# A decoder layer on one core: two output blocks by halves, a later conditioning product, and work moved to other phases

## The chip, the core and the metric

The kernel runs on one core of a Trainium2 chip. The core has TensorE (PE, with its weight loads shown apart as PEld), VectorE (DVE), ScalarE (ACT), GpSimd (POOL), SyncE (SP), which here issues most of the DMAs, and 16 DMA engines. Each engine takes its instructions in a fixed order, so an instruction that waits holds up all that stand behind it on that engine. The metric is the time of one execution on the device, in microseconds (us). The kernel before took 1681.6 us (median of 3 runs, 1681.38 to 1685.16).

## The reference

One layer of a decoder trunk is computed in float32 for 1024 prompt tokens and 8 requests of 8 tokens each, 1088 columns in all, with a model width of 1024:

```python
h = rms_norm(x, norm_mix) * (1 + sc) + sh            # sh, sc, gt = silu(c) @ w_ada_mix + b
P = h @ w_in                                         # RWKV-7, pooling and gate columns
merged = g_r * (rwkv(P) @ w_br_rwkv) + g_p * (pool(P) @ w_br_pool)
x = x + gt * (merged @ w_out)
sh, sc, gt = split(silu(c) @ w_ada_mlp + b_ada_mlp, 3)
h = rms_norm(x, norm_mlp) * (1 + sc) + sh
x = x + gt * (square(relu(h @ w_ff1)) @ w_ff2)
y = rms_norm(x, norm_final)
```

## The kernel before

Activations lie in SBUF with channels on the partitions and the 1088 columns along the free axis; a row of blocks (`xr[0]` to `xr[7]`) is the residual stream. HF is 544, half of the columns, HQ is 272. A float32 product is built from three matmuls of rounded operands: every operand is split into a high part (`whi`, or the first tile of a pair `mr`, `hx`, `t`), made by ACT with a copy, and a low part (`wlo`, or the second tile), made by DVE or POOL with a subtraction. ACT, DVE and POOL thus work ahead of PE all the time, and a PSUM tile is free for PE only after one of them has read ("evicted") it.

The first part of the program (to about 790 us) makes the first norm, `w_in`, the recurrent heads and the pooling. The change touches the second part, the function `phase2`, which goes through these stages.

- **Merge** (`or_job`, eight blocks m). DVE evicts the branch product into `t`, POOL adds the other branch (L1369), ACT and DVE split the sum into the pairs `mg` (L1372, L1373). POOL then writes one element of `t` into the next residual tile and into the first conditioning tiles (`behind`, L1338), so that their loads can't be issued before.
- **Output product** (`out_job(m, i)`, i the half of the columns). A job has two halves of weights; half 0 uses `mg[0]` to `mg[3]`, half 1 uses `mg[4]` to `mg[7]`, with 24 matmuls of 272 columns each. The list `order` sets the sequence: job 0 half 0, job 0 half 1, job 1 half 0, and so on.
- **Conditioning** (`ada`, `ada_part`, L290). `silu(c) @ w_ada_mlp` is made in three groups of four pairs of tiles `hid<-in_w_ada_mlp`, 512 KB a tile. Its matmuls (`wc<-hid,sT`, 8 a pair) are put between those of the output product by a planner (`Pace`), which counts modelled nanoseconds of matmuls: a first pair comes after `gap + lead`, each other one after `gap`.
- **ff1**, as a product of halves with seven terms c (0 to 6) in place of eight. Each output unit j is a "pair" `u`, `o`. For the first eight units (`early`) the terms 0 and 1 are computed ahead, while the norm still makes the operands of the other five; their `u` and `o` are parked in DRAM and come back later. In this early phase the order of terms is: c=0 of units j and j+1, then c=1 of both, and c=1 is added into the same PSUM tile that c=0 filled, after ACT has copied it to `u` (L1530). After c=1 ACT makes `o` by Relu and Square (L1532, L1533) before it is parked.
- **ff2**, in groups of units with phases `ph` 0 to 2, also with seven terms. `spread` loads and splits the operands of coming terms; DVE adds each PSUM tile into accumulators (L1697). Afterwards `whole` adds the accumulators into the residual stream (`residual`, L1876, L1879), and the last quarter of the units goes through eight plain jobs (`ff2_jobs`, 36 matmuls each, evicted by L1876 too), whose operands `hidden` splits (L1758). Their PSUM tiles lie where those of the sums lay.
- The last norm and the stores.

PE's order is written out by these lists and the planner. The order on the other engines comes from a scheduler that runs on modelled times when the program is built, so a moved line can change the order of its neighbours too.

Of the kernel before, what the change touches and what calls it, by code (L numbers as in the profile page):

```python
# [9 lines left out]
F32 = mybir.dt.float32  # L10
# [126 lines left out]
class K:  # L137
# [1060 lines left out]
    def run(self):  # L1198
        tc, nc, io = self.tc, self.nc, self.io
        with ExitStack() as ctx:  # L1200
            self.cp = ctx.enter_context(tc.tile_pool(name="cp", bufs=1))
            self.wp = ctx.enter_context(tc.tile_pool(name="wp", bufs=2))
            self.hx = ctx.enter_context(tc.tile_pool(name="hx", bufs=1))
            dp = ctx.enter_context(tc.tile_pool(name="dp", bufs=1, space=DRAM))
            scratch = lambda n, k: [dp.tile([P, NT], F32, name=f"{n}{i}") for i in range(k)]
            self.d_bv, self.d_y = (scratch(n, 4) for n in ("d_bv", "d_y"))
            self.d_or, self.d_op = ([scratch(n + s, 4) for s in "hl"] for n in ("d_or", "d_op"))
            self.d_th, self.d_x = scratch("d_th", 16), scratch("d_x", 14)
            self.d_xr, self.d_hid = scratch("d_xr", 8), scratch("d_hid", 8)
            cut = lambda n: [[dp.tile([P, HF], F32, name=f"{n}{c}_{j}") for j in range(4 * NG)] for c in range(7)]  # L1210
            self.d_ch, self.d_cl = cut("d_ch"), cut("d_cl")
            self.d_u = [dp.tile([P, HF], F32, name=f"d_u{j}") for j in range(NE)]
            self.pc = ctx.enter_context(tc.tile_pool(name="pc", bufs=2, space=PSUM))
            self.part = self.cp.tile([P, NPAR], F32, name="part")
            nc.gpsimd.dma_start(self.part, io["par"])
            self.kct = self.cp.tile([P, NKC], F32, name="kct")
            nc.gpsimd.dma_start(self.kct, io["kc"])
            self.eps = self.cp.tile([P, 3], F32, name="eps")
            for i, v in enumerate((NORM_EPS, KK_EPS, GN_EPS)):
                nc.gpsimd.memset(self.eps[:, i:i + 1], v)  # L1220
            self.hp = self.cp.tile([P, 16], F32, name="hp")
# [103 lines left out]
    def phase2(self):  # L1325
# [15 lines left out]
        def ada():  # L1341
# [7 lines left out]
            for g in range(3):  # L1349
# [2 lines left out]
                    self.done.add("ada")  # L1352
                    yield lambda: ("hid", NE - 1) in self.done
                asb = p.tile([P, 512], F32, tag="wr2", bufs=4, name=self.nm("asb"))
                yield from self.ada_part("w_ada_mlp", g, tile, asb, self.aq, "b_mlp", (8 * g, 8 * g + 4), 6200, 2500, 13000 if g == 0 else 0)

        def or_job(m):
            S = {}
# [7 lines left out]

            def after():
                t = S["t"]
                nc.gpsimd.tensor_tensor(t, t, S["u"], op=ALU.add)  # L1369
                hi, lo = zip(*[MR() for _ in range(2)])  # L1370
                for i, s in enumerate(split):
                    nc.scalar.activation(hi[i], t[:, s], AF.Copy)  # L1372
# [97 lines left out]
        def pair_steps(j, early):  # L1470
# [13 lines left out]
            def prep(c):  # L1484
                def go():
                    if c == 0:
                        return self.halves(raw("a", 0, 0), False)
                    if c == 5:
                        if early == 2:
                            raw("a", 0, 0)  # L1490
                            S["u"], S["o"] = self.pair(p, "hid", 4, dt=F32)
                            nc.sync.dma_start(S["u"], self.d_u[j])
                            nc.sync.dma_start(S["o"], self.d_ch[0][j])
                        b, cc = raw("b", 1, 0), raw("c", 1, 1)
                        nc.vector.tensor_tensor(cc, b, cc, op=ALU.add)
                        d = raw("d", None, None)
# [20 lines left out]
            def run(c):  # L1517
                def go(w):
                    if c in (0, 1):
# [3 lines left out]
                        if c == 0:  # L1523
                            if early:
                                S["u"], S["o"] = self.pair(p, "hid", 4, dt=F32)
                            else:
                                S["u"], S["u1"] = self.pair(self.hx, "hx", 16, dt=F32)
                                S["o0"] = HX(F32)
                                S["o"] = S["o0"][:, :HF]
                            nc.scalar.activation(v2(S["u"]), v, AF.Copy)  # L1530
                        else:
                            nc.scalar.activation(v2(S["o"]), v, AF.Relu)  # L1532
                            nc.scalar.activation(S["o"], S["o"], AF.Square)  # L1533
                            if early:
                                nc.sync.dma_start(self.d_u[j], S["u"])
                                nc.sync.dma_start(self.d_ch[0][j], S["o"])
                        return
                    ps = self.ps2()
                    yield from product(ps, c, w, True, True)
# [5 lines left out]
                        nc.vector.tensor_tensor(v2(S["u"]), v2(S["u"]), v, op=ALU.add)  # L1545
                    elif c == 6:
                        nc.vector.tensor_tensor(v2(S["u1"]), v2(S["u"]), v, op=ALU.add)
                    elif c == 4:
                        o = S["o1"] = HX(F32)
                        nc.vector.tensor_tensor(v2(S["u"]), v2(S["u"]), v, op=ALU.add)  # L1550
# [27 lines left out]
            def apart(c, x, hi):  # L1578

                if early:  # L1580
                    if c:
                        nc.sync.dma_start(self.d_ch[c][j], x)
                    return
                nc.scalar.activation(hi.bitcast(F32R), x, AF.Copy)
                nc.vector.tensor_tensor(x.bitcast(F32R), x, hi, op=ALU.subtract)
# [128 lines left out]
        def ff2():  # L1714
            n = 0
            for i, (g, ph, (_, run, c)) in enumerate(sums):
                n = n + 1 if i and sums[i - 1][1] == ph else 0
                yield from run(made.pop(0))
                more()
                if ph == 0 and n == 1:  # L1720
                    spread(g, (4,))
                if ph == 0 and n == 4:
                    spread(g, (3,))
                if ph == 1 and n in (2, 5):
                    if g in after:
                        spread(after[g], (n // 3,))
                    else:
                        for m in range(n // 3 * 4, n // 3 * 4 + 4):
                            self.xr[m] = HX(F32)
                            nc.sync.dma_start(self.xr[m], self.d_xr[m])  # L1730
                if ph == 2 and n in (0, 2, 4):
                    if g in after:
                        spread(after[g], ((6, 5, 2)[n // 2],))
                    elif n == 2:
                        hidden(6)

        def whole():

            yield lambda: "sums" in self.done
            for mp in range(4):  # L1740
                (a1, a4), (a2, a3) = ACC[mp]
                for i, s in enumerate(split):
                    c0, n = s.start, s.stop - s.start
                    for h in range(2):
                        x = (a1, a3)[h] if i == 0 else (a2, a4)[h]
                        if h != i:
                            nc.vector.tensor_tensor(x, a4, x, op=ALU.subtract)  # L1747
                        self.residual(self.xr[2 * mp + h], self.aq[:, 16 + 2 * mp + h, :])(c0, n, x)
                yield 1500

        hid = {}

        def hidden(grp):
            for j in range(4):
                raw, hi, lo = self.row(p, "hid", 4), self.row(p, "mr", 16, F32R), self.row(p, "mr", 16, F32R)
                nc.sync.dma_start(raw, self.d_hid[4 * (grp - 6) + j])
                nc.scalar.activation(hi, raw, AF.Copy)
# [10 lines left out]
        for m in range(8):  # L1768
            order += U(or_job(m))
        for i in range(2):  # L1770
            for m in range(8):
                order += U(out_job(m, i))
        order2 = []
        for m, j in enumerate(ff2_jobs(6)):
            order2 += U(j)
# [231 lines left out]
```

## Time and profile before

| | |
|---|---|
| time, median of 3 runs | 1681.6 us (1681.38 to 1685.16) |
| profiled execution, its own time | 1687.4 us |
| its span, from first to last instruction | 1685.6 us |
| PE, PEld busy | 1615.4 us (96%), 1501.4 us (89%) |
| DVE, ACT, POOL busy | 1023.3 us (61%), 677.3 us (40%), 358.5 us (21%) |
| mean granted TensorE clock | 0.982 |
| HBM traffic | 198.15 MB read, 76.72 MB written, 163 GB/s over the span |

PE is busy nearly all the time, so the time can change by what PE waits, by the time in which its clock is not granted in full (a matmul then shows about twice its pitch), and hardly by anything else. In the rows of the profile a group is given as line, engine, operation and `out<-in`; brackets behind a row of the timeline hold the idle time of that engine just before it and what ended it. In rows of windows the granted clock stands as PEclk, 1.00 in full.

### The profile page before, as it was taken

The page shows a single profiled execution, that of the slowest core. Times are in us where ns is not written, and L with a number is a line of the kernel's source. Part 1 is how long each engine was busy: PE and PEld are TensorE (multiplying, and loading weights), DVE is VectorE, ACT ScalarE, POOL GpSimd, SP SyncE. Part 2 cuts the span into 40 slices and gives each one's busy share as a digit, 9 for nine tenths or more (in the row PEclk, how much of TensorE's full clock was granted, in tenths as well). Part 3 has the DMA queues.
Part 4 walks back from the last instruction along what each step waited for, and adds up shares of the span by engine and source line. Part 5 has one row for each costly group of instructions (what it writes and reads, how often), then busy time and mean ns, then how long its engine had stood idle before and what let it go on. Part 6 is the DMA issues. An engine that isn't in the chain of part 4 may idle for free. (4 is left out here: it accounts for less than half of the span.)

```text
span 1685.6 us, 35156 instructions
## 1 busy us (share of the span) xinstructions
PE 1615.4 (96%) x14331; PEld 1501.4 (89%) x14331; DVE 1023.3 (61%) x1674; ACT 677.3 (40%) x1262; POOL 358.5 (21%) x393
## 2 busy tenths in 40 slices
PE   6999999998999999999989989999999999999997
PEld 3989878886888789979979989999999999999897
DVE  5686556845674456334635596776655577677646
ACT  4543333344334333422324374444555554333122
POOL 3310110010000000001722234453322141311221
PEclk9999999999998999999989999999999999999999
DMA  9233413232423242475964446766555876574112
GB/s 335 98 114 133 141 55 119 100 103 71 126 89 105 69 147 80 146 279 199 335 236 163 149 138 227 239 235 229 199 205 193 321 233 211 164 259 135 45 44 107
DMA packets 128321, 277.17 MB, mean 164 GB/s; under 512 B 16640, under 2 KB 30976, under 8 KB 128160
## 3 DMA queue, kind: packets, MB, share of 16 engines
q1 hardware_dynamic: 120480, 253.03, 44.0%
q10 hardware_dynamic: 6048, 16.23, 2.8%
q0 software_dynamic: 1632, 5.67, 1.0%
q8 instruction: 113, 1.85, 0.4%
q14 instruction: 48, 0.39, 0.1%
HBM read 198.15 MB, written 76.72 MB: 163 GB/s over the span
## 5 line engine op out<-in xcount | busy, mean ns | idle before, releaser
L170 PE MATMUL mm<-hx,whi 128*128 128x362 f32 (+1 forms) x1920 | 511.5, 348 | 6.9 <-ACT px L565 2.9
L170 PEld LDWEIGHTS mm<-hx,whi 128*128 128x128 f32 x1920 | 337.0, 192 | 43.5 <-issue 18.6
L170 PE MATMUL pr<-mr,whi 128*128 128x272 f32 x1792 | 338.9, 288 | 4.5 <-DVE hx L1697 3.4
L170 PE MATMUL mm<-hx,wlo 128*128 128x362 f32 (+1 forms) x960 | 317.6, 331 | 0.0
L170 PEld LDWEIGHTS pr<-mr,whi 128*128 128x128 f32 x1792 | 281.7, 189 | 8.6 <-issue 8.3
L170 PE MATMUL pr<-mr,wlo 128*128 128x272 f32 x896 | 258.5, 289 | 0.0
L193 ACT ACTIVATE whi<-wraw 128x512 fp32r<-128x512 f32 x201 | 126.4, 629 | 290.1 <-PE mm L170 109.3
L170 PEld LDWEIGHTS mm<-hx,wlo 128*128 128x128 f32 x960 | 184.5, 192 | 0.0
L194 DVE TENSOR_TENSOR wlo<-wraw,whi 128x512 fp32r<-128x512 f32 x146 | 112.2, 769 | 111.0 <-ACT whi L193 108.9
L170 PE MATMUL pr<-hx,whi 128*128 128x272 f32 x896 | 170.6, 289 | 6.4 <-ACT hid L1530 5.4
L170 PEld LDWEIGHTS pr<-mr,wlo 128*128 128x128 f32 x896 | 169.2, 189 | 0.0
L170 PE MATMUL mm<-mr,whi 128*128 128x272 f32 (+4 forms) x736 | 156.4, 307 | 6.5 <-DVE hx L1697 3.7
L170 PEld LDWEIGHTS pr<-hx,whi 128*128 128x128 f32 x896 | 141.7, 190 | 7.9 <-ACT hid L1530 5.7
L194 POOL TENSOR_TENSOR wlo<-wraw,whi 128x512 fp32r<-128x512 f32 x55 | 79.5, 1446 | 273.7 <-ACT whi L193 267.2
L170 PEld LDWEIGHTS mm<-mr,whi 128*128 128x128 f32 x736 | 121.4, 192 | 15.1 <-issue 7.3
L193 ACT ACTIVATE whi<-wr 128x512 fp32r<-128x512 f32 x123 | 76.3, 627 | 142.3 <-PE pr L170 118.2
L170 PE MATMUL pr<-hx,wlo 128*128 128x272 f32 x448 | 129.6, 289 | 0.0
L170 PE MATMUL mm<-mr,wlo 128*128 128x272 f32 (+4 forms) x368 | 111.7, 303 | 0.0
L170 PEld LDWEIGHTS pr<-hx,wlo 128*128 128x128 f32 x448 | 85.0, 190 | 0.0
L170 PE MATMUL pr<-t,whi 128*128 128x272 f32 x448 | 84.6, 287 | 0.0
L194 DVE TENSOR_TENSOR wlo<-wr,whi 128x512 fp32r<-128x512 f32 x94 | 70.3, 750 | 22.6 <-ACT whi L193 22.6
L170 PEld LDWEIGHTS mm<-mr,wlo 128*128 128x128 f32 x368 | 70.8, 193 | 0.2
(377 smaller groups left out, 2618.7 us busy)
## 6 DMA issues: line engine op xcount, KB each, us to landing
wr<-in_w_ff SPq DMA_DIRECT2D x123, 256.0 KB, 3.5
wraw<-in_w_ff SPq DMA_DIRECT2D x85, 256.0 KB, 3.1
hid<-d_ch SPq DMA_DIRECT2D x80, 272.0 KB, 4.4
wraw<-in_w_in SPq DMA_DIRECT2D x68, 256.0 KB, 3.0
d_ch<-hx SPq DMA_DIRECT2D x52, 272.0 KB, 4.3
hid<-in_w_ada_mlp SPq DMA_DIRECT2D x24, 512.0 KB, 5.7
d_th<-px SPq DMA_DIRECT2D x22, 544.0 KB, 3.0
wt<-d_x SPq DMA_DIRECT2D x20, 544.0 KB, 4.1
```

The lines of the kernel that those rows point to most:

```text
L170: return self.nc.tensor.matmul(out, lhsT, rhs, **kw)
L193: nc.scalar.activation(hi, raw, AF.Copy)
L194: (nc.gpsimd if pool else nc.vector).tensor_tensor(lo, raw, hi.bitcast(F32), op=ALU.subtract)
```

## The change

Five edits, all in `phase2`:

1. Output product of the first column half: jobs 0 and 1 run by halves (both jobs' half 0, then both jobs' half 1), and the last merge addition (m = 7) is on DVE in place of POOL.
2. Conditioning: the lead of the first pair becomes 19000 (was 13000), the gap of the others 5600 (was 6200).
3. Early units: after c=1 ACT only copies PSUM to `o`; `u` and `o` are both parked in a buffer of their own (`d_u[0]`, `d_u[1]`); Relu and Square are done when the unit has come back, at term 6, and the finished `o` is stored to `d_ch[0]` at the combinations (one store a unit more).
4. ff2: the term 2 of the coming operands is spread in phase 0 in place of the end of phase 2, the others at other counts, and the splits of the plain jobs' operands come in two parts.
5. `whole`: the additions into the residual stream take their factors from a copy `gq`, which is first written from a value of the last accumulator, so that none of them can run before the last sum.

```diff
@@ scratch in DRAM @@
-            self.d_u = [dp.tile([P, HF], F32, name=f"d_u{j}") for j in range(NE)]
+            self.d_u = [[dp.tile([P, HF], F32, name=f"d_u{i}_{j}") for j in range(NE)] for i in range(2)]
@@ ada @@
-                yield from self.ada_part("w_ada_mlp", g, tile, asb, self.aq, "b_mlp", (8 * g, 8 * g + 4), 6200, 2500, 13000 if g == 0 else 0)
+                yield from self.ada_part("w_ada_mlp", g, tile, asb, self.aq, "b_mlp", (8 * g, 8 * g + 4), 5600, 2500, 19000 if g == 0 else 0)
@@ or_job, after @@
-                nc.gpsimd.tensor_tensor(t, t, S["u"], op=ALU.add)
+                (nc.vector if m == 7 else nc.gpsimd).tensor_tensor(t, t, S["u"], op=ALU.add)
@@ pair_steps, prep of term 5 when a unit returns @@
-                            nc.sync.dma_start(S["u"], self.d_u[j])
-                            nc.sync.dma_start(S["o"], self.d_ch[0][j])
+                            nc.sync.dma_start(S["u"], self.d_u[0][j])
+                            nc.sync.dma_start(S["o"], self.d_u[1][j])
@@ pair_steps, run of terms 0 and 1 @@
+                        elif early:
+                            nc.scalar.activation(v2(S["o"]), v, AF.Copy)
+                            nc.sync.dma_start(self.d_u[0][j], S["u"])
+                            nc.sync.dma_start(self.d_u[1][j], S["o"])
                         else:
                             nc.scalar.activation(v2(S["o"]), v, AF.Relu)
                             nc.scalar.activation(S["o"], S["o"], AF.Square)
-                            if early:
-                                nc.sync.dma_start(self.d_u[j], S["u"])
-                                nc.sync.dma_start(self.d_ch[0][j], S["o"])
...
                     elif c == 6:
                         nc.vector.tensor_tensor(v2(S["u1"]), v2(S["u"]), v, op=ALU.add)
+                        if early:
+                            relu2(S["o"])
@@ apart @@
                 if early:
-                    if c:
-                        nc.sync.dma_start(self.d_ch[c][j], x)
+                    nc.sync.dma_start(self.d_ch[c][j], x)
                     return
@@ ff2 @@
-                if ph == 0 and n == 1:
-                    spread(g, (4,))
-                if ph == 0 and n == 4:
-                    spread(g, (3,))
+                if ph == 0 and n in (0, 2, 5) and (n or g != GO[0]):
+                    spread(g, ({0: 2, 2: 4, 5: 3}[n],))
...
-                if ph == 2 and n in (0, 2, 4):
+                if ph == 2 and n in (0, 4):
                     if g in after:
-                        spread(after[g], ((6, 5, 2)[n // 2],))
-                    elif n == 2:
-                        hidden(6)
+                        spread(after[g], (6 - n // 4,))
+                    else:
+                        hidden(6, n // 2)
@@ whole @@
+            gq = gt
+            nc.vector.tensor_copy(gq[:, 0, 0:1], ACC[3][1][1][:, 0:1])
+            nc.vector.tensor_copy(gq, self.aq[:, 16:24, :])
...
-                        self.residual(self.xr[2 * mp + h], self.aq[:, 16 + 2 * mp + h, :])(c0, n, x)
+                        self.residual(self.xr[2 * mp + h], gq[:, 2 * mp + h, :])(c0, n, x)
@@ the list order @@
         for i in range(2):
-            for m in range(8):
-                order += U(out_job(m, i))
+            outs = [out_job(m, i) for m in range(8)]
+            if i == 0:
+                order += [(j, h) for h in range(2) for j in outs[:2]]
+            for j in outs[0 if i else 2:]:
+                order += U(j)
```

SP's rows at the change from the merge to the output product, before (a load `wraw` is a block of output weights, a `hid` a tile of conditioning weights, `d_xr` the store of a residual block):

```order
L182 DMA wraw_9327<-in_w_out 128x512
L182 DMA wraw_9371<-in_w_out 128x512
L290 DMA hid_9282<-in_w_ada_mlp 128x1024
L290 DMA hid_9285<-in_w_ada_mlp 128x1024
L290 DMA hid_9358<-in_w_ada_mlp 128x1024
L290 DMA hid_9360<-in_w_ada_mlp 128x1024
L1407 DMA d_xr_120<-hx_8816 128x544
```

The same place on SP with the change:

```order
L182 DMA wraw_9327<-in_w_out 128x512
L290 DMA hid_9349<-in_w_ada_mlp 128x1024
L290 DMA hid_9352<-in_w_ada_mlp 128x1024
L182 DMA wraw_9367<-in_w_out 128x512
L182 DMA wraw_9401<-in_w_out 128x512
L290 DMA hid_9428<-in_w_ada_mlp 128x1024
L290 DMA hid_9430<-in_w_ada_mlp 128x1024
L1407 DMA d_xr_120<-hx_8824 128x544
```

The second pair of conditioning tiles stands one weight block earlier, and the third no longer directly behind it.

ACT's rows in the early phase of ff1, before (L1397 makes the high parts of the norm's operands, the two L1530 copy the c=0 products of units 4 and 5, for which PE waits before it adds c=1):

```order
L1397 ACTIVATE mr_10857<-hx_9064 128x544
L1397 ACTIVATE mr_10860<-hx_9134 128x544
L1397 ACTIVATE mr_10863<-hx_9196 128x544
L1397 ACTIVATE mr_10866<-hx_9258 128x544
L1397 ACTIVATE t_10890<-hx_9196 128x544
L193 ACTIVATE whi_10945<-wr_1490_10943 128x512
L1530 ACTIVATE hid_10941<-pr_10916 128x544
L193 ACTIVATE whi_10978<-wr_1495_10976 128x512
L1530 ACTIVATE hid_10974<-pr_10949 128x544
```

The same place on ACT with the change:

```order
L1530 ACTIVATE hid_10945<-pr_10920 128x544
L1397 ACTIVATE mr_10814<-hx_9010 128x544
L1397 ACTIVATE mr_10829<-hx_8824 128x544
L1397 ACTIVATE mr_10832<-hx_8886 128x544
L1397 ACTIVATE mr_10835<-hx_8948 128x544
L1397 ACTIVATE mr_10838<-hx_9010 128x544
L1397 ACTIVATE mr_10862<-hx_9072 128x544
L1397 ACTIVATE mr_10865<-hx_9142 128x544
L1397 ACTIVATE mr_10868<-hx_9204 128x544
L1397 ACTIVATE mr_10871<-hx_9266 128x544
L193 ACTIVATE whi_10982<-wr_1495_10980 128x512
L1530 ACTIVATE hid_10978<-pr_10953 128x544
```

Unit 4's copy now stands ahead of nine of the `mr` copies; unit 5's copy still stands behind them.

DVE's rows at the end of the sums, before (L1697 with `pr_17743` reads the last sum's PSUM, L1747 and L1876 are `whole`, L1876 on `mm` evicts the first plain job):

```order
L1876 SCALAR_TENSOR_TENSOR hx_17361<-hx_15006,aq,hx_17361 128x480
L1697 TENSOR_TENSOR hx_15006<-hx_15006,pr_17743 128x544
L1758 TENSOR_TENSOR mr_17948<-hid_17946,mr_17947 128x1088
L1876 SCALAR_TENSOR_TENSOR hx_17359<-hx_14951,aq,hx_17359 128x544
L1747 TENSOR_TENSOR hx_15006<-hx_15005,hx_15006 128x544
L1876 SCALAR_TENSOR_TENSOR hx_17363<-hx_15006,aq,hx_17363 128x544
L1876 SCALAR_TENSOR_TENSOR hx_17249<-mm_17841,aq,hx_17249 128x364
```

The same place with the change (the lines L1699, L1750, L1761, L1882, L1885 are the old L1697, L1747, L1758, L1876, L1879), first from the last sum on, then up to the first job:

```order
L1699 TENSOR_TENSOR hx_15012<-hx_15012,pr_17767 128x544
L1761 TENSOR_TENSOR mr_17974<-hid_17972,mr_17973 128x1088
L1741 COPY gt_8733<-hx_15012 128x1
L1742 COPY gt_8733<-aq 128x72
L1750 TENSOR_TENSOR hx_15012<-hx_15011,hx_15012 128x544
L1882 SCALAR_TENSOR_TENSOR hx_17273<-hx_14826,gt_8733,hx_17273 128x544
L1882 SCALAR_TENSOR_TENSOR hx_17275<-hx_14827,gt_8733,hx_17275 128x544
```

```order
L1882 SCALAR_TENSOR_TENSOR hx_17387<-hx_15012,gt_8733,hx_17387 128x544
L1882 SCALAR_TENSOR_TENSOR hx_17385<-hx_15012,gt_8733,hx_17385 128x480
L1885 TENSOR_TENSOR rs_17902<-hx_14861,gt_8733 128x64
L1882 SCALAR_TENSOR_TENSOR hx_17273<-mm_17865,aq,hx_17273 128x364
L1885 TENSOR_TENSOR rs_17906<-hx_14860,gt_8733 128x64
L194 TENSOR_TENSOR wlo_17945<-wraw_17942,whi_17944 128x512
L1882 SCALAR_TENSOR_TENSOR hx_17273<-mm_17866,aq,hx_17273 128x362
```

Before, two additions of `whole` stand between the last sum and the first job's eviction; now 15 of its 16 do (eight of 544 columns, seven of 480), with three of the small products `rs`.

More of the change, by code (lines that the diff above doesn't have):

```diff
@@ L1747, in whole, with hidden @@
                             nc.vector.tensor_tensor(x, a4, x, op=ALU.subtract)
-                        self.residual(self.xr[2 * mp + h], self.aq[:, 16 + 2 * mp + h, :])(c0, n, x)
+                        self.residual(self.xr[2 * mp + h], gq[:, 2 * mp + h, :])(c0, n, x)
                 yield 1500
         hid = {}
-        def hidden(grp):
-            for j in range(4):
+        def hidden(grp, part=None):
+            for j in range(4) if part is None else (part, part + 1):
                 raw, hi, lo = self.row(p, "hid", 4), self.row(p, "mr", 16, F32R), self.row(p, "mr", 16, F32R)
```

## The prediction

> **What bounds the kernel.** I read the busy shares first, then what PE waited for, then PE's clock by windows, and last the timeline of each place that the diff touches.
>
> ```profile
> PE 1615.4 (96%) x14331; PEld 1501.4 (89%) x14331; DVE 1023.3 (61%) x1674; ACT 677.3 (40%) x1262; POOL 358.5 (21%) x393
> ```
>
> ```profile
> PE mm L170 <- DVE sq L408: 14.0, 2, 12.0
> ...
> PE pr L170 <- ACT hid L1530: 5.4, 1, 5.4
> ...
> PE mm L170 <- DVE hx L1697: 3.7, 1, 3.7
> PE pr L170 <- DVE hx L1697: 3.6, 6, 1.9
> ...
> PE mm L170 <- ACT mr L1372: 2.7, 1, 2.7
> ...
> PE wc L170 <- DMA hid<-in_w_ada_mlp: 1.8, 1, 1.8
> ```
>
> PE is busy for 96% of the span, so its waits and its clock are what can change. The longest wait (L408, 14.0 us) belongs to the start, which no edit touches. The other five rows are phase 2, 17.2 us, and the edits stand at four of them: at 2.7 and 1.8 (place A, output product), 5.4 (place B, early ff1) and 3.7 (place D, end of ff2). The 3.6 us are spread over ff2 (place C).
>
> ```profile
> core 0: us, PE busy (x) PEld busy (x) DVE busy (x) ACT busy (x) POOL busy (x), PEclk, DMA share, GB/s
> ...
> 845.00:849.00 4.00, 2.06 (x7) 1.76 (x8) 3.44 (x4) 1.36 (x3) 2.36 (x5) 0.70 0.33 119
> 849.00:853.00 4.00, 3.43 (x16) 3.11 (x14) 0.50 (x1) 1.13 (x2) 1.27 (x1) 0.50 0.99 381
> ...
> 996.00:1000.00 4.00, 3.73 (x16) 3.73 (x17) 4.00 (x8) 1.79 (x4) 0.00 (x0) 0.50 0.38 143
> ```
>
> A wait costs twice here: behind the waits of places A and B the clock is granted at 0.50 (PEclk) for whole windows of 4 us, so a wait that goes takes the half clock with it.
>
> **The change, part by part. Place A.** PE's own rows, then who keeps it:
>
> ```profile
> 839.49 1.07 PE L170 MATMUL wc<-hid,sT 128*32 128x512 f32 x8
> 840.49 0.52 PE L170 MATMUL mm<-mr,whi 128*128 128x272 f32 x2
> ...
> 843.83 0.29 PE L170 MATMUL mm<-mr,wlo 128*128 128x272 f32 x1
> 846.77 0.60 PE L170 MATMUL mm<-mr,whi 128*128 128x272 f32 x1 [2.65 <-ACT mr L1372]
> ...
> 854.18 2.98 PE L170 MATMUL wc<-hid,sT 128*32 128x512 f32 x8 [1.75 <-DMA hid<-in_w_ada_mlp]
> 857.09 0.52 PE L170 MATMUL mm<-mr,whi 128*128 128x272 f32 x2
> ```
>
> ```profile
> 843.06 2.97 POOL L1369 TENSOR_TENSOR t<-t,t 128x1088 f32<-128x1088 f32 x1
> ```
>
> ```profile
> 841.87 1.82 DVE L1373 TENSOR_TENSOR mr<-t,mr 128x544 fp32r<-128x544 f32 x1
> ```
>
> ```profile
> 847.33 1.93 SPq L290 DMA_DIRECT2D hid<-in_w_ada_mlp  x4
> ```
>
> ```profile
> DMA to landing us min/median/max: 3.6/5.5/10.2
> ```
>
> At full clock a matmul of 272 columns follows the last by 0.125 us (27 of them start from 840.49 to 843.83, the first of these steps a little longer), and a pair of conditioning tiles takes 1.00 (839.49 to 840.49). PE stood still from 843.96; 24 matmuls (3.0) and one pair (1.0) later it would be at 847.95, and was there at 857.09: 9.1 us lost. With the change, 24 matmuls of job 1 stand in front of the first use of `mg[7]`, so that is due at 843.96 + 3.0 = 846.95. DVE makes the addition when L1373 ends (843.69); its price isn't in the trace, between a DVE subtraction of as many columns (1.28, L1758 at place D) and POOL's 2.97, and I take 1.3, since nothing on POOL runs beside it: 845.0, and the split 0.7 later: in time, by 1.3 us. Then `behind` lets SP issue the second pair of tiles about 1.1 earlier than 847.33 (POOL's addition ended at 846.03, DVE's will at 845.0), two tiles in place of four. The lines for these loads (min, median, longest) give a landing 5.5 later, 851.7, or 10.2 later, 856.4. The planner's new numbers put the first pair 45 matmuls later and this one another 45: 839.49 + 90 x 0.125 + 1.0 = 851.7. I leave 0.6 of wait for what lands beside it: gain 8.5, between 9.1 and, with the longest landing (4.7 late, and 1.4 at half clock, as estimated at B), 3. Later pairs are due 5.6 + 1.0 apart (45 matmuls and a pair) and are issued two pairs ahead, 13 us for a landing of 10.2 at most: nothing.
>
> **Place B.**
>
> ```profile
> 989.62 5.03 ACT L1397 ACTIVATE mr<-hx 128x544 fp32r<-128x544 f32 x9
> ...
> 995.61 0.61 ACT L1530 ACTIVATE hid<-pr 128x544 f32<-128x544 f32 x1
> ```
>
> ```profile
> 990.55 0.29 PE L170 MATMUL pr<-hx,wlo 128*128 128x272 f32 x1
> 996.27 0.82 PE L170 MATMUL pr<-hx,whi 128*128 128x272 f32 x2 [5.44 <-ACT hid L1530]
> ```
>
> PE's product c=1 of unit 4 waited for L1530, which stood behind nine copies on ACT. Now it stands ahead of them, and four Squares (0.65 each) have left the queue: I put its end at 991.2, a wait of 0.4. But unit 5's copy is still behind the nine (5.03), a `whi` and itself (0.5 each): 997.3, while PE, with 24 matmuls in between, is there at 994.2. So 3.1 us of wait are left of 5.4, and most of the half clock (3.7 busy us at 0.50 in the window from 996 us lost 1.9; I take 1.4 of it as left, since the wait is shorter): before 5.4 + 1.9, now 0.4 + 3.1 + 1.4, a gain of 2.4. If ACT reaches both in time the gain is 7.3; if its copies wait for DVE (4.00 of 4.00 busy in the window from 996 us), 0.
>
> The four Squares, and four from the later units, don't vanish: eight Relus and eight Squares come back when the units return, with eight more stores.
>
> ```profile
> L193 ACT ACTIVATE whi<-wraw 128x512 fp32r<-128x512 f32 x12 | 7.6, 632 | 14.6 <-PE pr L170 14.6
> ```
>
> ```profile
> DMA to landing us min/median/max: 2.0/4.6/6.1
> ```
>
> The first line is of the stretch from 1004 to 1100 us, the second of the loads of `d_u` there (min, median, longest). ACT idles 14.6 us ahead of that one group, so 8 x 1.3 = 10.5 us of Relu and Square fit. But by the order Relu of a returning `o` stands ahead of older work (Relu of the unit in process, then the next `whi`), so ACT waits up to 4.6 us a unit for the landing. Its cover: ACT waits for PE to free a `whi` (14.6 us), so it splits at once, four buffers ahead, three products or 9 us before use. 4.6 + 1.3 is less than 9: nothing. Gone, it would cost what the slower rival below says. The stores queue on SP ahead of weight loads that wait for a buffer anyway: nothing.
>
> **Place C.** The spreads are written elsewhere, but in the order they stay where they were, apart from a swap of neighbours on SP, ACT and DVE: nothing, at most 0.5 either way. The waits of 3.6 us stay.
>
> **Place D.**
>
> ```profile
> 1573.37 0.78 PE L170 MATMUL mm<-mr,whi 128*128 128x362 f32 x2 [3.68 <-DVE hx L1697]
> ```
>
> ```profile
> 1568.00:1572.00 4.00, 1.69 (x13) 1.38 (x11) 4.00 (x5) 1.73 (x3) 1.76 (x1) 1.00 0.19 68
> 1572.00:1576.00 4.00, 2.63 (x9) 2.63 (x10) 3.96 (x6) 0.00 (x0) 0.17 (x1) 0.70 0.21 66
> 1576.00:1580.00 4.00, 4.00 (x23) 4.00 (x23) 0.97 (x2) 0.00 (x0) 0.00 (x0) 0.87 0.00 0
> ...
> 1552.00:1572.00 20.00, 8.49 (x10) 1.00 0.16 54
> ```
>
> ```profile
> L1758 DVE TENSOR_TENSOR mr<-hid,mr 128x1088 fp32r<-128x1088 f32 x7 | 9.0, 1282 | 0.0
> ...
> L1876 DVE SCALAR_TENSOR_TENSOR hx<-hx,aq,hx 128x480 f32<-128x480 f32 x8 | 7.6, 962 | 0.0
> ...
> L1876 DVE SCALAR_TENSOR_TENSOR hx<-hx,aq,hx 128x544 f32<-128x544 f32 x4 | 3.1, 776 | 0.0
> ```
>
> ```profile
> 1555.27 0.35 DVE L1879 TENSOR_TENSOR rs<-hx,aq 128x64 f32<-128x64 f32 x2
> 1555.54 0.71 DVE L1697 TENSOR_TENSOR hx<-hx,pr 128x544 f32<-128x544 f32 x1
> ...
> 1556.77 0.71 DVE L1876 SCALAR_TENSOR_TENSOR hx<-hx,aq,hx 128x480 f32<-128x480 f32 x1
> ...
> 1579.69 1.10 DVE L1876 SCALAR_TENSOR_TENSOR hx<-mm,aq,hx 128x364 f32<-128x364 f32 x2 [3.02 <-PE mm L170]
> ...
> 1585.64 1.10 DVE L1876 SCALAR_TENSOR_TENSOR hx<-mm,aq,hx 128x364 f32<-128x364 f32 x2 [3.00 <-PE mm L170]
> ```
>
> DVE is full up to 1576 (the last row is L1876 alone: 8.5 of the 20 us from 1552 to 1572 are `whole`), and PE waits for its last L1697. With L1876 moved behind it, DVE keeps pace, and PE goes on at 1570.1, when its last sum is done and added: 3.3 for the wait, 1.7 for the half clock (0.30 and 0.13 of 4 us missing in the two windows), 0.2 for a small one before, 5.2 gained. But PE now fills PSUM for jobs 0 and 1 and needs job 0's tiles for job 2, 11.4 us later (two jobs of 5.95, the distance of the last two rows, less three matmuls that it has issued before). Until DVE reads them, it makes one L1758 (1.28), one L1747 (0.71), 15 additions (eight at 0.77, seven at 0.71) and three `rs` (0.18): 13.7, less 0.07 for each start ahead of the last end (1555.54 against 1555.62), 12.4, and 1.0 more for those that POOL slows (962 ns is the mean of eight at 480 columns): job 0's first tile is read by 1584.1, its third 1.8 later, behind a `wlo` and an `rs`. PE is there at 1581.5 and waits 2.6 + 0.6, with 1.2 of half clock (a little less than at B, since it falls into pieces). Net gain 0.8, between -1.5 (all 480-column additions at the mean of 0.96) and 5.2.
>
> Sum: 8.5 + 2.4 + 0 + 0.8 = 11.7. The profiled execution took 1687.4 (1685.6 of span and 1.8 around it), so it would take 1675.7; against the median of 1681.6, 5.8 lower, the forecast is 1669.9, said as 1670.
>
> A rule that bears on it: the Trainium skill, page "TensorE: Matmul & The Clock Gate", Part 1, puts PE at half rate after an idle window of some 3.4 us, and its practical rule is to have no PE gap above that. The trace here shows 0.50 after gaps of 2.65 and 1.75 with work between them, so I go by the rows. By that rule the shortened waits at B and D would cost no clock, and the time would be 1667.
>
> **Rivals.** (1) Slower: the landing of the returning units stops ACT, and what it holds back is late at PE. For it: the Relus stand ahead of the `whi` copies. Against: 9 us of cover. Uncovered, each of eight units costs 4.6: 36.8 - 11.7 = 25 slower, 1707; from 2.1 a unit on (16.7 in all) the kernel is slower than before by over 0.3%. (2) The second conditioning pair lands late after all, by the longest row: A gains 3 and the time is 1675.5. For it: the DMA share of 0.99 around it; against: only two tiles are sent first. (3) Unit 5's copy is in time too: B gains 7.3, 4.9 more, 1665. The order speaks against it. (4) B doesn't do what it says, since ACT waits for DVE's operands before the copies: 1672. (5) The shortened waits at B and D leave the clock in full, 1.4 + 1.2 more: 1667. The rows of half clock above speak against it.
>
> **The numbers.** Forecast 0.46; rivals 1: 0.11, 2: 0.16, 3: 0.12, 4: 0.10, 5: 0.05. This kernel's runs tell about 0.3% (5 us) from no change: faster is under 1676.6, slower over 1686.6. Half of rival 2 lies within it: faster 0.81, same 0.08, slower 0.11. Range: from 1664 (3, with D at its best a little lower) to 1679 (2, with D at its worst); what is left out is the slower rival and the ends where several bounds meet.
>
> **What would show it.** A: no wait on L1372, the clock at 1.00 from 845 to 857, a wait on `hid<-in_w_ada_mlp` under 1 us. B: one wait on L1530 of some 3 us in place of 5.4. D: no wait on the last L1699, a new one of PE at the third job on DVE's L1882. The prediction is wrong if PE waits between 1010 and 1140 us for `whi` or `wlo`, or for a conditioning pair at all of its later places.

## The result

The changed kernel takes 1684.83 us (median of 14 runs, 1679.35 to 1689.41), the kernel before 1684.15 us (median of 14 runs, 1681.38 to 1689.3): a ratio of 1.0001 with a 95% interval of 0.9989 to 1.0014. The forecast was 1670, with a range of 1664 to 1679. The change gains and loses in equal parts.

The page of the changed kernel, its first line, and what PE waited for (microseconds in total, times, longest):

```profile
PE 1615.6 (96%) x14331; PEld 1503.0 (89%) x14331; DVE 1018.9 (61%) x1677; ACT 680.5 (40%) x1270; POOL 356.3 (21%) x392
```

```profile
PE pr L170 <- DVE hx L1566: 6.0, 4, 3.0
...
PE mm L170 <- DVE hx L1882: 3.6, 2, 2.5
PE pr L170 <- ACT hid L1530: 3.3, 2, 2.7
PE w L170 <- DVE rs L1885: 2.1, 1, 2.1
...
PE mm L170 <- DVE hx L1699: 0.4, 1, 0.4
```

The waits on L1372 and on the conditioning tiles are gone, the one on L1530 fell from 5.4 to 3.3, and the one on the last sum (L1697, now L1699) from 3.7 to 0.4. In their place stand L1566, L1882 and L1885, 11.7 us together, which the kernel before did not have. L1566 is the eviction of term 3 of an early unit that has come back (L1563 before). Windows of the changed kernel (before the last three numbers PE, PEld, DVE, ACT and POOL busy; these three are PEclk, the share of the DMA engines and GB/s):

```profile
845.00:849.00 4.00, 4.00 (x33) 3.01 (x32) 2.52 (x5) 1.84 (x3) 1.99 (x5) 1.00 0.64 182
849.00:853.00 4.00, 4.00 (x34) 4.00 (x33) 0.77 (x2) 0.66 (x1) 0.67 (x1) 1.00 1.00 398
...
1056.00:1060.00 4.00, 1.03 (x8) 0.84 (x7) 3.92 (x5) 0.30 (x1) 3.13 (x2) 1.00 0.18 71
1060.00:1064.00 4.00, 4.00 (x23) 4.00 (x23) 4.00 (x5) 2.06 (x4) 3.69 (x3) 0.63 0.95 300
...
1580.00:1584.00 4.00, 1.76 (x5) 1.31 (x6) 3.44 (x11) 0.00 (x0) 1.15 (x4) 0.50 0.40 126
1584.00:1588.00 4.00, 4.00 (x18) 4.00 (x17) 0.36 (x2) 0.00 (x0) 0.70 (x3) 0.66 0.01 4
```

```profile
1092.00:1096.00 4.00, 2.11 (x15) 2.00 (x14) 3.96 (x5) 2.05 (x4) 4.00 (x3) 0.90 0.51 180
1096.00:1100.00 4.00, 4.00 (x24) 4.00 (x24) 3.62 (x5) 0.94 (x2) 1.92 (x2) 0.67 0.94 287
```

At the output product the clock is now full and PE without a gap. Half clock stands in new places, behind the new waits: near 1061 us, near 1095 us (0.10 and 0.33 of 4 us missing, 1.7 us in all) and near 1580 us.

PE makes the same number of matmuls, 14331, in every kernel here, so two traces can be laid side by side by the number of the matmul, and the starts compared. (Edits 1 and 2 change the order inside the stretches; at the border 10420 some conditioning matmuls trade places with neighbours, which moves it by under 0.4 us.) Between the matmuls 8000, 9000, 9390, 10420, 13560 and 13800 (826, 965, 1021, 1152, 1549 and 1589 us in the kernel before) lie the places of the prediction; each entry is how much longer (+) or shorter (-) the stretch took than in the kernel before, one profiled execution each. The last stretch ends with the last matmul. The profiled execution of the kernel before took 1687.4 us, 3 more than the median of its 14 runs, so the entries lean to the minus side:

| kernel | to 826, no edit there | A: output product, norm | B: early units | their return | rest of ff1, ff2 (C) | D: end of the sums | rest | all |
|---|---|---|---|---|---|---|---|---|
| forecast | 0 | -8.5 | -2.4 | 0 | 0 | -0.8 | 0 | -11.7 |
| changed kernel | +1.3 | -9.6 | -2.1 | +8.6 | -3.5 | +2.9 | 0.0 | -2.3 |
| e1 | -5.7 | -7.9 | -2.1 | +3.7 | -3.1 | +3.0 | +0.4 | -11.8 |
| e2 | -1.2 | -6.7 | +0.6 | +2.5 | -2.8 | +2.8 | +0.1 | -4.6 |
| e3 | -1.5 | -6.6 | -3.7 | +9.3 | -2.3 | -0.2 | 0.0 | -4.9 |
| e4 | -5.4 | -6.1 | -0.5 | +4.2 | -2.0 | -0.1 | +0.1 | -9.7 |
| e5 | -9.0 | -7.9 | -2.1 | +2.9 | -1.4 | -5.5 | 0.0 | -23.0 |
| e6 | -2.0 | +0.1 | -2.1 | +8.9 | -1.7 | -0.3 | 0.0 | +2.9 |
| e7 | -8.9 | +0.4 | -0.3 | +0.6 | -2.9 | +0.8 | +0.1 | -10.1 |
| e8 | -0.4 | -1.6 | +0.8 | +0.1 | -4.1 | +0.6 | +0.1 | -4.5 |
| e9 | -3.3 | -2.9 | -0.3 | +1.8 | -3.5 | +0.5 | +0.1 | -7.5 |
| e10 | -4.7 | -6.2 | +0.4 | +1.0 | -1.3 | -5.6 | 0.0 | -16.5 |

The first column is a warning. No edit stands there (in e5 the orders of PE, DVE, POOL and SP are those of the kernel before, and among ACT's rows one load has moved), and the stretch still differs by up to 10 us from one execution to another (last section). So a stretch with a window of half clock in or out (some 1.7 us each, as in the rows at 1095 us) is uncertain by 2 or 3 us (e9, without edits 1 to 3, took 2.9 less at A), and conclusions rest on what repeats in several rows: the return costs 8.6, 9.3 and 8.9 in the three kernels that have edit 3 as it is, and the end of the sums takes 2.8 to 3.0 more in the three that have edit 5 as it is.

### The profile page after: what moved, and what is told of

The parts are those of the page before. It is cut to its first block, busy times and chain, and to the rows that moved or that the text cites. A ratio compares the mean times of both kernels' runs of the same rounds, so it can differ in the third digit from the quotient of the medians.

```text
span 1683.1 us, 35182 instructions
## 1 busy us (share of the span) xinstructions
PE 1615.6 (96%) x14331; PEld 1503.0 (89%) x14331; DVE 1018.9 (61%) x1677; ACT 680.5 (40%) x1270; POOL 356.3 (21%) x392
## 5 line engine op out<-in xcount | busy, mean ns | idle before, releaser
L1699 DVE TENSOR_TENSOR hx<-hx,pr 128x544 f32<-128x544 f32 x68 | 48.7, 716 | 42.4 <-PE pr L170 42.1
```

The lines of the kernel that those rows point to most:

```text
L1699: nc.vector.tensor_tensor(acc, acc, v, op=ALU.add)
```

## The experiments

**e1. Who holds up the return.** In the changed kernel SP, ACT and DVE stand like this ahead of PE's longest wait on L1566 (three timelines of one place, then PE):

```profile
1045.30 0.79 SPq L1493 DMA_DIRECT2D hid<-d_u  x1
1046.13 1.49 SPq L1481 DMA_DIRECT2D wr<-in_w_ff  x2
1051.31 0.33 SPq L1584 DMA_DIRECT2D d_ch<-hid  x1
1052.04 0.33 SPq L1481 DMA_DIRECT2D wraw<-in_w_ff  x1
```

```profile
1049.94 0.66 ACT L1514 ACTIVATE hid<-hid 128x544 f32<-128x544 f32 x1 [4.44 <-DMA wr<-in_w_ff]
1050.63 0.66 ACT L1515 ACTIVATE hid<-hid 128x544 f32<-128x544 f32 x1
```

```profile
1053.08 0.69 DVE L194 TENSOR_TENSOR wlo<-wr,whi 128x512 fp32r<-128x512 f32 x1 [4.44 <-ACT whi L193]
1056.04 0.69 DVE L1495 TENSOR_TENSOR wr<-wraw,wr 128x512 f32<-128x512 f32 x1 [2.27 <-DMA wraw<-in_w_ff]
...
1058.96 0.71 DVE L1566 TENSOR_TENSOR hx<-hx,pr 128x544 f32<-128x544 f32 x1
```

```profile
1059.81 0.48 PE L170 MATMUL pr<-mr,whi 128*128 128x272 f32 x2 [2.97 <-DVE hx L1566]
```

ACT waits for the returned half, makes Relu and Square until 1051.29, and only then can SP issue the store of that half (1051.31). The weight load `wraw` stands behind the store and goes out at 1052.04, 4.4 us after the two loads ahead of it were issued (1046.13 + 1.49). (The profile names a weight load as what ended ACT's wait of 4.44; for the other waits of L1514 it names the load of the half, below.) DVE's L1495 waits for it, and the eviction L1566 stands behind L1495. In the kernel before such loads follow each other at once:

```profile
1041.53 0.33 SPq L1481 DMA_DIRECT2D wr<-in_w_ff  x1
1042.24 0.33 SPq L1481 DMA_DIRECT2D wraw<-in_w_ff  x1
```

So two things could hold the return up: ACT itself (DVE's first row waits 4.44 us for a `whi` that ACT makes after its Relu and Square), or SP behind ACT. e1 takes the stores out of SP's queue and leaves ACT's wait.

```diff
                 if early:
-                    nc.sync.dma_start(self.d_ch[c][j], x)
+                    (nc.sync if c else nc.scalar).dma_start(self.d_ch[c][j], x)
                     return
```

> The changed kernel with one thing altered: the stores of the returned halves (d_ch[0] of the early units) are issued by ACT and no longer stand in SP's queue. Theory (SP): those stores wait on SP for ACT's Square, and the weight loads behind them go out late, so DVE's line L1495 waits for its weights, and the eviction L1566 stands behind it. Then PE's waits on L1566 between 1010 and 1140 us fall from 6.0 us to under 1.5, no window of half clock is left there, and the time is 7 to 9 us under that of the changed kernel, about 0.9955 of the kernel before. Rival (ACT): it is ACT itself that is held by the landing of the returned halves, and its splits come late whatever SP does. Then the waits on L1566 stay above 4 us and the time within 2 us of the changed kernel, 1.000 of the kernel before.

Measured: 1679.77 us, 0.9982 (0.9967 to 0.9996) of the kernel before. SP's rows at the same place in e1, the `wraw` now directly behind the two loads:

```profile
1040.49 1.35 SPq L1481 DMA_DIRECT2D wr<-in_w_ff  x2
1042.21 0.33 SPq L1481 DMA_DIRECT2D wraw<-in_w_ff  x1
```

What PE waited for in e1, and below it ACT's wait for the returned halves, in the changed kernel and in e1:

```profile
PE pr L170 <- DVE hx L1566: 3.6, 5, 1.7
```

```profile
ACT hid L1514 <- DMA hid<-d_u: 13.8, 5, 4.5
```

```profile
ACT hid L1514 <- DMA hid<-d_u: 15.8, 6, 5.3
```

ACT waits as long as in the changed kernel, yet the return costs 3.7 in place of 8.6, and 2.9 in e5: SP's queue carried some 5 us of it. Of these, 2.4 are PE's wait on L1566 (6.0 to 3.6), and most of the rest are the two windows of half clock behind it: in e1 the clock was at 1.00 from 1040 to 1120 us. So the theory is right on SP, but not on all of it: it put the waits at under 1.5 us and the gain at 7 to 9, and the interval takes in neither its ratio of 0.9955 nor the rival's 1.000. ACT holds DVE up as well. These are DVE's waits for ACT's `whi` from 1000 to 1140 us in the changed kernel, in e1, and in e2, where Relu and Square are back in front of the parking:

```profile
DVE wlo L194 <- ACT whi L193: 14.0, 6, 4.5
```

```profile
DVE wlo L194 <- ACT whi L193: 12.2, 7, 4.9
```

```profile
DVE wlo L194 <- ACT whi L193: 7.9, 9, 2.2
```

They hardly fall with the stores out of SP's way and fall by about 6 us without edit 3. That these waits make up the 3.6 us that stayed is likely, but no run shows it alone.

**e2. Without edit 3.** The changed kernel, with the activation of the early units back ahead of the parking.

```diff
...
-                        elif early:
-                            nc.scalar.activation(v2(S["o"]), v, AF.Copy)
-                            nc.sync.dma_start(self.d_u[0][j], S["u"])
-                            nc.sync.dma_start(self.d_u[1][j], S["o"])
                         else:
                             nc.scalar.activation(v2(S["o"]), v, AF.Relu)
                             nc.scalar.activation(S["o"], S["o"], AF.Square)
+                            if early:
+                                nc.sync.dma_start(self.d_u[j], S["u"])
+                                nc.sync.dma_start(self.d_ch[0][j], S["o"])
...
-                        if early:
-                            relu2(S["o"])
...
```

> The changed kernel with edit 3 undone (activation of the early units before they are parked, as before). Theory: the 6.0 us of waits on L1566 and two windows of half clock (3.4) go, and at the early units PE waits for L1530 as before (5.4 and 3.4 of half clock in place of 3.3 and 1.7): 9.4 - 3.8, so 5 to 6.5 us faster than the changed kernel, about 0.9965 of the kernel before. Rival: the waits between 1010 and 1140 us come from PE arriving there 10 us earlier (edits 1 and 2) than DVE and the loads can follow; then they stay at 4 us or more, on L1563 or a neighbour, and the time is that of the changed kernel or above it.

Measured: 1681.53 us, 0.9988 (0.9973 to 1.0003). The wait on L1530 is back, that at the return nearly gone (in windows from 830 to 1600 us):

```profile
PE pr L170 <- ACT hid L1530: 5.4, 1, 5.4
...
PE pr L170 <- DVE hid L1545: 1.2, 4, 0.3
PE pr L170 <- DVE hx L1563: 1.0, 2, 0.6
```

The return still took 2.5 us more than in the kernel before, so the rival may have a share: PE comes there some 6 us earlier, and DVE has less in hand. In e4 that was 4.2, in e10 1.0, and in e9, where PE is 3 us early, 1.8. By the stretches e2 gains 6.1 us at the return on the changed kernel and loses 2.7 at the early units, 3.4 where 5 to 6.5 were expected. By the whole time it can't be told from the changed kernel.

**e3. Without edit 5.**

```diff
-            gq = gt
-            nc.vector.tensor_copy(gq[:, 0, 0:1], ACC[3][1][1][:, 0:1])
-            nc.vector.tensor_copy(gq, self.aq[:, 16:24, :])
...
-                        self.residual(self.xr[2 * mp + h], gq[:, 2 * mp + h, :])(c0, n, x)
+                        self.residual(self.xr[2 * mp + h], self.aq[:, 16 + 2 * mp + h, :])(c0, n, x)
```

> The changed kernel with edit 5 undone (the additions of the accumulators run as soon as they can). Theory: edit 5 moved DVE work from under the sums to behind them, where PE needs the first jobs' PSUM tiles, and costs more (waits of 0.4 + 5.7 and 3.4 of half clock) than it saves (3.7 + 0.3 + 1.7): without it 3 to 4 us faster than the changed kernel, 0.998 of the kernel before, and a wait of about 3.7 us on the last L1697 comes back. Rival: with edit 4 DVE has become fuller ahead of the last sums, so that the old order now waits longer there: no gain, 1.000.

Measured: 1682.75 us, 0.9991 (0.9972 to 1.001). At the end of the sums it took 0.2 us less than the kernel before, in place of 2.9 more, and the wait of old is back:

```profile
PE mm L170 <- DVE hx L1699: 3.7, 1, 3.7
```

So edit 5 costs 3 us as it is, as the theory said; the whole times of e3 and of the changed kernel can't be told apart.

**e4. Edits 1 and 2 alone**, in the kernel before (the lines of the diff on `ada`, `or_job` and the list `order`).

> The kernel before with edits 1 and 2 alone (output blocks by halves, addition on DVE, conditioning later). Theory: 9 us are gained between 840 and 860 us and kept to the end, since what follows is a chain of PE: 0.9945 of the kernel before. Rival: the gain is given back at the early units, where ACT and DVE were late already (5.4 us of wait on L1530): PE comes 9 us earlier and waits there up to 9 us longer; then the time is 0.997 to 1.000 of the kernel before.

Measured: 1677.0 us, 0.9974 (0.9956 to 0.9991). Most of place A is gained (6.1 us), and the early units give nothing back (-0.5): the rival fails in its place. But 4.2 us are given back later, at the return, by ten waits of up to 0.7 us, so the gain isn't kept to the end as the theory had it, and the time lies where the rival put it:

```profile
PE pr L170 <- DVE hid L1545: 1.8, 6, 0.3
PE mm L170 <- DVE t L1365: 1.8, 1, 1.8
PE pr L170 <- DVE hx L1563: 1.8, 4, 0.7
```

The middle row is a wait that the prediction didn't have: the first matmuls of the output product need PSUM tiles that L1365 of the last merge block still reads. It measured 0.4 to 1.8 us in six of the seven kernels with edits 1 and 2; the changed kernel has none there.

**e6. Edit 3 alone**, in the kernel before.

> The kernel before with edit 3 alone. Theory: SP's hold behind the stores makes DVE late by some 4 us a unit whoever comes early, and PE waits on L1566 for 3 us or more in all between 1010 and 1150 us. Rival: DVE has that much slack while PE isn't early (edits 1 and 2 bring it 9 us earlier): under 1.5 us of waits there. Either way the early units gain 2 to 2.5 us (wait on L1530 of some 3.3 in place of 5.4).

Measured, one run: 1690.34 us (before: 1682.41, median of 11). The return costs 8.9 us with PE only 2 us early, so it is edit 3 that makes it late, and an earlier PE isn't needed for that:

```profile
PE pr L170 <- DVE hx L1566: 6.2, 4, 3.2
```

Alone it gains 2.1 at the early units and loses four times that.

**e7 and e8. Edit 1 alone and edit 2 alone**, in the kernel before.

> The kernel before with edit 1 alone (blocks by halves, addition on DVE), conditioning where it was. Theory: edit 1 takes the wait of 2.7 us on L1372, but the second conditioning pair is then due 4 us before its tiles can land, so that a wait of 3 to 5 us on them and a window of half clock stand in its place: of the 9 us, 2 to 4 are gained. Rival: the wait on L1372 alone is what starts the half clock, and without it the tiles land in time: 7 us or more.

> The kernel before with edit 2 alone (conditioning later). Theory: the wait on the conditioning tiles (1.8) goes and with it part of the half clock, the wait of 2.7 us on L1372 stays with one window of half clock: of the 9 us, 3 to 5.5 are gained. Rival: with the pair gone from in front of it, PE comes to the last block 1 us earlier and waits the longer, 3.7 and two windows: under 2 us gained.

Measured, one run each: 1676.96 and 1682.63 us (before: 1682.41, median of 11); by stretches, place A took 0.4 us more with edit 1 alone and 1.6 less with edit 2 alone. (e7's time is low by the first stretch, -8.9, where no edit stands.) What PE waited for, first e7, then e8:

```profile
PE wc L170 <- DMA hid<-in_w_ada_mlp: 5.1, 2, 4.5
```

```profile
PE mm L170 <- ACT mr L1372: 4.0, 1, 4.0
```

Each edit by itself only hands the wait on: to the conditioning tiles, which then come 5.1 us late, or to the last merge block, 4.0 in place of 2.7. For e7 both guesses were too high, for e8 its rival is right. The gain at A (6.1 to 9.6 us in seven kernels with both) belongs to the two together.

**e9. Edit 4 alone**, in the kernel before.

> The kernel before with edit 4 alone (spreads at other counts). Theory: a swap of neighbours on DVE puts an eviction L1697 ahead of a split, and the wait of PE at the third stretch of ff2 (1.94 us before) falls to 0.8 to 1.4 us; no more than 1 us in all is gained between 1152 and 1549 us of the kernel before, if no window of half clock falls there. Rival: the 3.5 us that the changed kernel gained between these places come from the edit, and 2.5 us or more show here.

Measured, one run: 1679.56 us (before: 1684.45, median of 11). The stretch C took 3.5 us less, as the rival said, since the wait of 1.94 us at 1464 us was down to 0.2 and the window of half clock behind it absent. But this is not shown to be the edit: without edit 4 the same wait was 1.95 in e4 and e6, 1.3 in e7 and 0.2 in e8, and with it 0.2 in e9, 0.8 in the changed kernel and in e2, 1.3 and 1.4 in e3 and e1, 1.8 and 1.9 in e5 and e10. And e8, without edit 4, took 4.1 us less at C. Whether edit 4 does anything stays open.

**e5. What would keep the gains.** The stores on ACT as in e1, and edit 5 for the last two of the four accumulator groups only.

```diff
-                        self.residual(self.xr[2 * mp + h], gq[:, 2 * mp + h, :])(c0, n, x)
+                        self.residual(self.xr[2 * mp + h], (gq[:, 2 * mp + h, :] if mp >= 2 else self.aq[:, 16 + 2 * mp + h, :]))(c0, n, x)
```

> The changed kernel with the stores of the returned halves on ACT's queue, as in e1, and edit 5 for half of the additions only: those of the first two accumulator groups (8 of 16) run under the sums as before, those of the last two wait for the last sum. Theory: what edit 5 costs is the amount of DVE work between the last sum and the first job's eviction against the 11.4 us that PE has in two jobs' PSUM tiles; eight additions (some 9 us with what stands beside them) fit, so the new waits on L1882 and L1885 (5.7 us) and their half clock are gone and the wait on the last L1699 stays under 2 us. At the end of the sums 3 to 5 us less than before, in all 10 to 13 us under the kernel before: 0.9925 to 0.994. Rival: any additions behind the last sum come in PE's way, since the evictions are queued after them: a wait of 2 us and more at the third job remains, and the whole gains no more than 7 us, 0.996.

Measured: 1668.27 us (median of 6, 1663.26 to 1673.16), 0.9917 (0.9893 to 0.9942) of the kernel before. DVE's rows at the end of the sums in e5, and PE's:

```profile
1551.13 0.71 DVE L1699 TENSOR_TENSOR hx<-hx,pr 128x544 f32<-128x544 f32 x1
...
1557.74 2.86 DVE L1882 SCALAR_TENSOR_TENSOR hx<-hx,gt,hx 128x544 f32<-128x544 f32 x4
1560.53 1.08 DVE L1882 SCALAR_TENSOR_TENSOR hx<-mm,aq,hx 128x364 f32<-128x364 f32 x2
```

```profile
1551.90 0.59 PE L170 MATMUL mm<-mr,whi 128*128 128x362 f32 x2 [0.42 <-DVE hx L1699]
```

PE goes on at 1551.9, and DVE comes to the first job's tiles at 1560.53, 8.6 us later and within the 11.4 that PE has. No wait follows, and the stretch takes 5.5 us less than before. That is the gain of 5.2 which the prediction named for the wait that goes, here without the new one. The slowest of e5's six runs (1673.16) is faster than the fastest of the kernel before beside it (1678.69) and of the changed kernel (1679.35, measured at another time). The gain of 0.8% is a little more than the 0.6 to 0.75% that were expected.

**e10. e5 without edit 3** (edits 1, 2, 4 and half of 5).

> The kernel of e5 with edit 3 undone, that is edits 1, 2, 4 and half of edit 5. Theory: edit 3 gains 2 us at the early units and, with its stores out of SP's way, costs 0 to 1.5 us later against the old activation: without it the time is within 3 us of e5, on its slower side, 0.992 to 0.995 of the kernel before. Rival: even with the stores on ACT the wait of ACT for the returned halves costs more than the early units gain: then 1 to 3 us faster than e5, 0.989 to 0.991.

Measured: 1672.37 us, 0.9936 (0.9912 to 0.9961). By stretches, edit 3 with its stores on ACT gains 2.5 us at the early units (-2.1 against +0.4) and costs 1.9 at the return (+2.9 against +1.0), so what it is worth lies within what these runs can tell; the intervals of e5 and e10 overlap.

## Why the prediction was wrong

- **Place A, -8.5: right.** Measured -9.6, and -6.1 to -9.6 in the kernels with both edits. The clock was at 1.00 from 845 to 857 us and no wait on L1372 or on the conditioning tiles stayed. How near the number came is in part luck: the 9.1 us that could be lost were read from one execution, and e9, with the old code at A, took 2.9 us less there. The working didn't name the wait on L1365.
- **Place B, -2.4: right**, in its parts too: 0.6 and 2.7 us of wait on L1530 (forecast 0.4 and 3.1) and one window of half clock, together -2.1.
- **The return, 0: wrong, and this step failed the prediction.** The sentence was "The stores queue on SP ahead of weight loads that wait for a buffer anyway: nothing." It gives no row for this. A load does go out late in the kernel before (`wr` at 1049.62, 7.4 us after the load ahead of it), but the `wraw` at 1042.24 goes out at once behind another load. With the store of a returned half in front, such a load waited for ACT, which waited for a landing, and DVE's queue carried that to L1566: +8.6 us. In it are 6.0 us of waits on L1566 and two windows of half clock, some 3.4 us, for which the term of nothing had no place either (0.6 us of small waits went). The cover of 9 us that was counted belonged to ACT's splits. PE itself waited for no `whi` or `wlo`, so the sign that was named for this failure didn't show; but DVE did wait for ACT's `whi` (14.0 us, 7.9 in e2), and with the stores elsewhere the return took 2.9 to 3.7 more than before, against 1.0 to 4.2 with the old activation. Rival 1 had the place and the sign, and ACT held by the landing; most of the cost came by another path, SP's queue, and at 1.1 us a unit in place of 4.6.
- **Place C, 0:** measured -3.5, of which nothing is shown to be the edit (e9).
- **Place D, -0.8: the sign was wrong, mostly by one term.** DVE came to the first job's tiles 13.4 us after PE had gone on (1564.10 and 1577.53), much as forecast. PE's rows at the third job in the changed kernel, and DVE's rows ahead of the last of them:

```profile
1578.26 0.57 PE L170 MATMUL mm<-mr,whi 128*128 128x364 f32 x2 [2.50 <-DVE hx L1882]
...
1580.13 0.97 PE L170 MATMUL mm<-mr,whi 128*128 128x362 f32 x2 [1.13 <-DVE hx L1882]
...
1583.52 0.94 PE L170 MATMUL w<-mr,whi 128*128 128x362 f32 x2 [2.11 <-DVE rs L1885]
```

```profile
1580.00 0.51 DVE L1882 SCALAR_TENSOR_TENSOR hx<-w,aq,hx 128x298 f32<-128x298 f32 x1
...
1582.51 0.34 DVE L1885 TENSOR_TENSOR rs<-hx,gt 128x64 f32<-128x64 f32 x2
1583.14 0.22 DVE L1885 TENSOR_TENSOR rs<-w,aq 128x64 f32<-128x64 f32 x1 [0.30 <-POOL hx L1887]
```

  The first wait was forecast as 2.6 and is 2.50. What follows it was put at 0.6 and is 3.24 (1.13 and 2.11): the second tile stands behind an `rs` and a `wlo` that take 0.79 and 0.82 us, where others take 0.21 and 0.68 (POOL is busy at the time, 3.35 us of the 4 from 1576; whether that slows them, no run tests), and the `w` tile, read at 1580.00, is read once more by an `rs` of its own, which stands behind the second job's evictions and two other `rs` and comes at 1583.14. The half clock was put at 1.2 and is about 2.2 (in the two windows shown above 1.76 us of work at 0.50, which is 0.9 lost, and 0.34 of 4 us missing). So the stretch took 2.9 more, where 0.8 less was forecast. By the rule of the Trainium skill, page "TensorE: Matmul & The Clock Gate", Part 1, gaps of 1.1 to 2.5 us would have cost no clock; the row of 0.50 decides against it here, as in the prediction.
- The sum: -9.6 - 2.1 + 8.6 + 2.9 is about 0 without C and the chance of the clock at the start, which is what the medians say. The base was off too: 1681.6 was the median of 3 runs, and 14 give 1684.15, which is 2.5 of the 15 us between forecast and result.

## What to carry to other kernels

A store that is added to a queue can make the loads behind it wait for what the store waits for (here 4.4 us for one load). Follow that chain to its end (here SP, ACT, a landing, DVE, PE), and test the claim that the loads wait anyway on each load behind the store, not on one. Work that is moved behind a stretch has to fit into what its consumer has in buffers (here 11.4 us of PE in PSUM tiles): half of it moved, 8.6 us of DVE ahead of the first tile, gained 5.5 us; all of it, 13.4 us, lost 2.9. And two edits at one place can each be worth 0 to 2 us alone and 6 to 10 together, when each only uncovers the other's wait.

## What the runs showed of the hardware

The same instructions took up to 10 us more or less in the first 826 us from execution to execution (first column of the table), and most of the difference lies in windows of half clock: in the traces' records of the granted clock these add up to 30.7 us in the kernel before and 17.1 in e5, which is worth about 7 of the 9 us between them. In all these traces a stretch of half clock is 3.4, 6.8 or 10.2 us long, but for the one at the program's end. One of them, in the kernel before and at the same work in e5:

```profile
520.00:524.00 4.00, 3.71 (x23) 3.53 (x23) 0.60 (x2) 3.65 (x6) 0.00 (x0) 0.79 0.05 17
524.00:528.00 4.00, 4.00 (x70) 3.00 (x69) 0.61 (x2) 2.88 (x6) 0.00 (x0) 0.50 0.03 5
528.00:532.00 4.00, 4.00 (x14) 3.62 (x13) 0.59 (x1) 0.66 (x2) 0.00 (x0) 0.50 0.55 185
```

```profile
516.00:520.00 4.00, 4.00 (x55) 3.00 (x56) 0.31 (x2) 3.56 (x7) 0.00 (x0) 0.57 0.00 0
520.00:524.00 4.00, 4.00 (x65) 3.64 (x60) 1.25 (x3) 1.74 (x3) 0.00 (x0) 1.00 0.41 136
```

In the one the clock is low for some 10 us, in the other for under 4; what decides between the two, no run here shows. This spread is larger than most of the single terms of the change, so its parts could only be read by stretches of the same matmuls in several kernels, and not from the times.
